# Two of four key blocks of the first attention turned by VectorE and through DRAM, and twelve weight units split in the first down-projection

## The chip, the cores and the metric

The kernel runs on one core of a Trainium2 chip. A core has a matrix engine (TensorE, PE in the profile; PEld is its loading of weights), VectorE (DVE), ScalarE (ACT), GpSimd (POOL), and SyncE (SP), which here only starts DMA transfers. Each engine works through its own list of instructions and waits for the others at semaphores. The metric is the device time of one execution in microseconds (us); lower is better.

## The reference

Two sequences of 512 tokens of width 1024 go through one encoder layer. Cut to what matters here:

```python
x = x + 0.5 * swiglu(rms_norm(x, ffn1_norm), w_gate, w_up, w_down)     # d_ff 2816
h = rms_norm(x, mix_norm)
aq, ak, av, mq, mk, mv, gate_pre, o_pre, g_att, g_mlstm = split(h @ w_in)
s = einsum('bqkgd,bskd->bkgqs', q, k) * scale                          # 8 heads, 512 x 512 each
p = softmax(s, axis=-1)
att = einsum('bkgqs,bskd->bqkgd', p, v)
mem = mlstm_bidirectional(mq, mk, mv, gate_pre, o_pre)                 # 4 heads
merged = sigmoid(g_att) * (att @ w_up_att) + sigmoid(g_mlstm) * (mem @ w_up_mlstm)
x = x + merged @ w_out
x = x + 0.5 * swiglu(rms_norm(x, ffn2_norm), ...)                      # then a last rms_norm
```

## The kernel before

All large products are done with operands split in two: a rounded value `hi` and a remainder `lo = x - hi`; a product is three matmuls (hi hi, hi lo, lo hi). So each weight that comes from DRAM is split first: ScalarE copies it to `hi`, VectorE subtracts to get `lo`. A *weight unit* is 128 columns of `w_in` over all 1024 rows, 512 KB; its split is one ScalarE and one VectorE instruction on 128x1024 elements (`split_w`, L278 and L279). `load_w` does this on the first use of a unit, and writes `hi` and `lo` to DRAM (`wpark`, twice 512 KB); on a later use under the same key in `parked` it loads both from there and splits nothing.

The program runs: first gate and up projection, first down-projection (`ffn_down`), `mix(0, ...)` for the first sequence, `mix(1, ...)` for the second, and the second feed-forward block. `ffn_down` works in 28 steps. Steps 0 to 13 and 21 to 27 have 36 matmuls of 128x512, steps 14 to 20 have 24. In each, four PSUM banks are filled one after the other (`d` from 0 to 3), and each is read out by one ScalarE or VectorE instruction (`flush_`, L663, L665). Four banks hold the X group (`mm`, `mm`, `mm`, `pso`) and four the Y group (`pss`, `pss`, `pst`, `pst`), so the next step of the same group can only start on a bank when its last flush is done. `prep` splits the weights of the step two further on (L715, L716).

`mix` has the attention. `score` makes one 128x512 block of probabilities: matmuls (L1101), a maximum (L1104), the exponential (L1106), the reciprocal (L1107), and the scaling of the rows, on ScalarE (L1109) or on VectorE (L1111). `values` multiplies them with V, for which each probability block must be turned, keys to the partitions. In `mix(0)`, `turn_keys` does this for all four key blocks with four TensorE transposes each (L1117) and a split of the result (`parts`). In `mix(1)` only key blocks 2 and 3 go this way. Blocks 0 and 1 are turned in 32x32 squares by VectorE (`turn_early`, L1129) into `turned`, which is rows 0 and 1 of the `box` tile; SP writes them to DRAM (`send`, L1133, `abuf`), and POOL's queue reads them back a head later in the order that completes the turn (`fetch`, L1138). `among(n)` puts `n` matmuls of waiting weight units between these steps. Twelve units of 24 matmuls each are used up in this way: those of `mem_qk(1, .)`, `att_gate(0)` to `att_gate(5)` and `out_gate(0)` to `out_gate(3)`.

The order on each engine is fixed when the program is built, by a scheduler that sorts by priority (program order, moved by `shifted`) and by what it takes to be ready; `pin` keeps marked instructions in program order.

Of the kernel before, what the change touches and what calls it, by code (L numbers as in the profile page):

```python
# [8 lines left out]
F32 = mybir.dt.float32  # L9
F32R = mybir.dt.float32r  # L10
# [16 lines left out]
def encoder(ctx, tc, I, outs):  # L27
# [519 lines left out]

    def ffn_down(wd, rb, ring, tail, xres, done, at_step, hook, turned=None):
# [4 lines left out]
        e5 = A([P, DH, S], F32, "e5")  # L553
        right = [[t[:, q] for q in range(3)] for t in rt] + [[t[:, 3] for t in rt]]
# [5 lines left out]
        s1s = ring.rows["s"]  # L560
        at = [0, 0]

        def load_right(i):
# [144 lines left out]

    def normed(xt, g, R, d):
# [138 lines left out]
    def mix(s, xh, xl, early=None, extra=None, after=None):  # L848
# [248 lines left out]
        def score(h, b):  # L1097
            hk = h // 4
            p = PS()
            for j in range(2):  # L1100
                pin(nc.tensor.matmul(p, qT[:, h, b * P:(b + 1) * P], kv[:, hk * 2 + j, :],  # L1101
                                     start=(j == 0), stop=(j == 1)))
# [4 lines left out]
            V_.reciprocal(c[:, 2:3], c[:, 1:2])  # L1107
            if b % 2 and (s or h or b < 3):
                nc.scalar.activation(e, e, AF.Copy, scale=c[:, 2:3])  # L1109
            else:  # L1110
                V_.tensor_scalar(e, e, c[:, 2:3], None, op0=ALU.mult)  # L1111
            return e

        def turn_keys(Ps, kb):
            p = PT()
            for b in range(4):
                pin(nc.tensor.transpose(p[:, b * P:(b + 1) * P], Ps[b][:, kb * P:(kb + 1) * P], ident))  # L1117
            return parts(p.rearrange("p (i a m) -> p a i m", i=4, a=4) if s else p)

# [21 lines left out]
        pos = {}  # L1141
        KBS = (2, 3, 0, 1) if s else (0, 1, 2, 3)

        def values(h, kb, pp):
# [5 lines left out]
            if kb != KBS[3]:  # L1150
                return
            po = pos.pop(h)
            order = ((lambda t: t.rearrange("p (a i m) -> p i a m", i=4, a=4)),
                     (lambda t: t.rearrange("p (i a m) -> p i a m", i=4, a=4))) if s else (lambda t: t,) * 2
            if h % 2 == 0:
# [30 lines left out]
        for b in range(4):  # L1186
            Ps.append(score(0, b))
            next(rope, None)
            among(FIRST[b])
        if s:  # L1190
            for i in range(2):
                turn_early(Ps[i], i)
        last = None
        for h in range(HA):
            nxt = []
            for b in range(4):
# [8 lines left out]
                if h + 1 < HA:  # L1205
                    nxt.append(score(h + 1, b))
                if s and (h, b) != (HA - 1, 3) and b in (3, 0):
                    if b == 3:
                        for i in range(2):
                            turn_early(nxt[i], i)  # L1210
                    else:
                        for i in range(2, 4):
                            turn_early(Ps[i], i)
                if s and b == 1:
                    send(h)
                n0, n1_ = FILLER if b else SOON
                among(n0)
                pp = None
                if not s or b > 1:
                    pp = h, b, turn_keys(Ps, b)  # L1220
# [8 lines left out]
            Ps = nxt  # L1229
        for b in range(2 * s):  # L1230
            pp = HA - 1, b, fetch(HA - 1, b)
# [520 lines left out]

    ffn_down(I["ffn1_w_down"][0], rbuf[0], up.ring, tail, xbuf, done1, 7, mix_consts)

# [201 lines left out]
```

## Time and profile before

| | us |
|---|---|
| median of 3 runs (2034.21 to 2035.5) | 2035.04 |
| profiled execution, its own time | 2037.6 |
| its span, first to last instruction | 2035.8 |
| first gate and up projection, about | 0 to 437 |
| first down-projection | 437 to 640 |
| `mix(0)` up to its attention | 640 to 705 |
| attention of `mix(0)`, first to last score matmul (L1101) | 705 to 803 |
| attention of `mix(1)`, up to its last score matmul | to 1169 |

The granted clock of TensorE is 0.999 over the span. The profile has no instruction of `fetch`, `send` or `turn_early` ahead of 1080 us: in the kernel before only `mix(1)` uses them. In rows of the profile a time in front is the start within the span; "x4" counts instructions; a bracket says how long the engine was idle before the row and whose instruction ended the wait.

### The profile page before, as it was taken

The numbers are of one execution on the slowest core, as the hardware profiler recorded it, in microseconds if no ns is written. First come the engines' busy times: TensorE is split into PE (matmuls) and PEld (weight loads), VectorE is DVE, ScalarE is ACT, GpSimd is POOL, SyncE is SP. The second block draws the span as 40 slices with busy tenths as digits, with TensorE's granted clock in tenths as the row PEclk, the third lists the DMA queues.
The fourth block names the chain that finished last, engine by engine and source line by source line (L and its number), as shares of the span: only waits on it lengthen the run. The fifth ranks groups of instructions, "written<-read, shape, count | busy, mean of one in ns | idle before, by whom it ended". The sixth has DMA issues, their size and how long they took to land.

```text
span 2035.8 us, 26777 instructions
## 1 busy us (share of the span) xinstructions
PE 2020.2 (99%) x9185; PEld 1665.7 (82%) x9185; DVE 1584.0 (78%) x2828; ACT 921.5 (45%) x1675; POOL 111.1 (5%) x148
## 2 busy tenths in 40 slices
PE   9999999999999999999999999999999999999998
PEld 7888888888888888888888877888888888888887
DVE  7988888886797798776566867467798988786797
ACT  7644444442234577653325654245444444442224
POOL 0000000001003000100120000011000000000001
PEclk9999999999999999999999999999999999999999
DMA  9656565799766954868656668877565655689753
GB/s 312 197 171 216 177 218 182 237 334 364 271 214 225 294 169 148 259 208 302 211 166 209 214 189 268 274 228 228 173 206 166 217 177 179 205 332 352 269 196 119
DMA packets 334696, 462.17 MB, mean 227 GB/s; under 512 B 21384, under 2 KB 207840, under 8 KB 333280
## 3 DMA queue, kind: packets, MB, share of 16 engines
q1 hardware_dynamic: 329920, 446.08, 65.8%
q0 software_dynamic: 4480, 14.11, 2.0%
q8 instruction: 72, 1.18, 0.2%
q14 instruction: 64, 0.52, 0.1%
q10 hardware_dynamic: 160, 0.27, 0.0%
HBM read 292.44 MB, written 167.94 MB: 226 GB/s over the span
## 4 chain that ended last, share of the span: by engine, by line
PE 91%; DVE 3%; DMA 3%; ACT 2%; issue 1%; SPq 0%; DVEq 0%; ACTq 0%
PE mm L839 13%; PE pso L374 12%; PE pst L374 12%; PE mm L374 10%; PE mm L632 9%; PE pss L374 6%; PE pst L632 4%; PE pss L632 4%; PE mm L825 4%; PE mm L804 3%; PE pso L632 3%; PE pso L1148 1%; PE pss L1101 1%; PE pst L839 1%; PE pss L839 1%; PE pso L1360 1%
## 5 line engine op out<-in xcount | busy, mean ns | idle before, releaser
L374 PE MATMUL pst<-xc,w 128*128 128x512 f32 x1056 | 253.8, 389 | 1.2 <-ACT t L409 1.2
L374 PEld LDWEIGHTS pst<-xc,w 128*128 128x128 f32 x1056 | 198.1, 188 | 42.7 <-ACT t L409 1.6
L374 PE MATMUL mm<-xc,w 128*128 128x512 f32 x972 | 229.6, 390 | 1.6 <-ACT f L382 1.6
L374 PEld LDWEIGHTS mm<-xc,w 128*128 128x128 f32 x972 | 182.0, 188 | 39.6 <-ACT f L382 2.1
L632 PE MATMUL mm<-rt,w 128*128 128x512 f32 x765 | 178.7, 389 | 0.0
L839 PE MATMUL mm<-xh,w 128*128 128x512 f32 x560 | 176.1, 391 | 1.4 <-DMA w<-wpark 1.4
L332 ACT ACTIVATE w<-t 128x512 fp32r<-128x512 f32 x176 | 106.5, 627 | 135.7 <-issue 63.1
L632 PEld LDWEIGHTS mm<-rt,w 128*128 128x128 f32 x765 | 143.5, 188 | 29.8
L333 DVE TENSOR_TENSOR w<-t,w 128x512 fp32r<-128x512 f32 x176 | 117.8, 688 | 40.9 <-ACT w L332 39.1
L374 PE MATMUL pso<-xc,f 128*128 128x512 f32 x528 | 127.0, 389 | 0.0
L374 PE MATMUL pss<-xc,w 128*128 128x512 f32 x528 | 126.8, 389 | 0.0
L374 PE MATMUL pso<-xc,w 128*128 128x512 f32 x528 | 126.8, 389 | 0.0
L839 PEld LDWEIGHTS mm<-xh,w 128*128 128x128 f32 x560 | 104.8, 188 | 23.7 <-DMA w<-wpark 1.8
L374 PEld LDWEIGHTS pso<-xc,f 128*128 128x128 f32 x528 | 99.0, 188 | 21.0 <-DVE t L413 0.4
L374 PEld LDWEIGHTS pso<-xc,w 128*128 128x128 f32 x528 | 99.1, 188 | 20.6
L374 PEld LDWEIGHTS pss<-xc,w 128*128 128x128 f32 x528 | 99.1, 188 | 20.6
L825 PE MATMUL mm<-xh,w 128*128 128x512 f32 x336 | 111.9, 398 | 0.0
L839 PE MATMUL mm<-xl,w 128*128 128x512 f32 x280 | 109.6, 391 | 0.0
L715 ACT ACTIVATE w<-wr 128x512 fp32r<-128x512 f32 x72 | 45.1, 632 | 138.4 <-PE pso L632 64.8
L278 ACT ACTIVATE w<-wr 128x1024 fp32r<-128x1024 f32 (+1 forms) x64 | 65.3, 1030 | 80.4 <-issue 24.5
L279 DVE TENSOR_TENSOR w<-wr,w 128x1024 fp32r<-128x1024 f32 (+1 forms) x64 | 79.8, 1247 | 26.6 <-ACT w L278 15.7
L715 ACT ACTIVATE w<-t 128x512 fp32r<-128x512 f32 x82 | 51.8, 632 | 107.4 <-PE pst L632 62.4
(457 smaller groups left out, 4080.4 us busy)
## 6 DMA issues: line engine op xcount, KB each, us to landing
rt<-rbuf SPq DMA_DIRECT2D x154, 512.0 KB, 5.4
wpark<-w SPq DMA_DIRECT2D x88, 512.0 KB, 3.6
w<-wpark SPq DMA_DIRECT2D x88, 512.0 KB, 5.3
wr<-in_ffn_w_gate_dram SPq DMA_DIRECT2D x62, 512.0 KB, 5.4
rbuf<-tab SPq DMA_DIRECT2D x102, 256.0 KB, 4.0
wr<-in_ffn_w_up_dram SPq DMA_DIRECT2D x44, 512.0 KB, 4.6
rbuf<-f SPq DMA_DIRECT2D x72, 256.0 KB, 4.2
wr<-in_w_in_dram SPq DMA_DIRECT2D x36, 512.0 KB, 5.7
```

The costliest lines, as they stand in the source:

```text
L278: pin(nc.scalar.activation(hi, raw, AF.Copy))
L279: pin(lo_eng.tensor_tensor(lo, raw, f(hi), op=ALU.subtract))
L332: pin(nc.scalar.activation(t[:, 0], src, AF.Copy))
L333: pin(V_.tensor_tensor(t[:, 1], src, f(t[:, 0]), op=ALU.subtract))
L374: nc.tensor.matmul(p, a[:, k, :], xt[:, b, k, :], start=(first and k == 0 and i == 0), stop=(k == HK_ - 1 and i == 2), skip_group_check=True)
L632: nc.tensor.matmul(p, u[:, a, d * P:(d + 1) * P], r[:, b, ts], start=(first and q == 0 and k == 0), stop=(q == len(us) - 1 and k == 2), sk ...
L715: nc.scalar.activation(hi, src, AF.Copy)
L804: mark(nc.tensor.matmul(p[b][:, :N], a[:, k, bs], w_[:, kl, :], start=(k == 0 and i == 0), stop=(k == KD - 1 and i == 2)), (kl, b, i) == ( ...
L825: pin(nc.tensor.matmul(p[0], a[:, k, :], b, start=(k == 0 and i == 0), stop=(k == n - 1 and i == 2)))
L839: mark(nc.tensor.matmul(p, a[:, k, :], b, start=(k == 0 and i == 0), stop=last), last)
L1101: pin(nc.tensor.matmul(p, qT[:, h, b * P:(b + 1) * P], kv[:, hk * 2 + j, :], start=(j == 0), stop=(j == 1)))
L1148: pin(nc.tensor.matmul(pos[h], Vst[:, kb, h // 4, :], w, start=(kb == KBS[0] and i == 0), stop=(kb == KBS[3] and i == 1)))
```

## The change

In `mix(0)` key blocks 0 and 1 now go the way that they go in `mix(1)`, and the blocks are taken in the order 2, 3, 0, 1. From its second head on, all rows of `mix(0)` are scaled on ScalarE. And `ffn_down` gets a list `aside` of twelve weight units of `w_in`: the ones named above. The half of the tile `e5` that was unused holds one unit at a time (`spare`: `lo` and `hi`). `split_aside` loads a unit on POOL's queue, splits it on ScalarE (L569) and VectorE (L570), and writes both halves to `wpark` on POOL's queue (L574). The unit is entered in `parked`, so that `mix(0)` loads it split. One unit is written into the program after each step from 10 on. Only the first `ffn_down` gets a list.

```diff
+        e5_ = A([P, KD, S], F32, "e5")
+        e5, spare = e5_[:, 0:DH], e5_[:, DH:KD].rearrange("p (i a) c -> p i (a c)", i=2)
...
+        def split_aside(view, key):
+            lo, hi = [spare[:, i].rearrange("p (k c) -> p k c", c=view.shape[2]) for i in range(2)]
+            nc.gpsimd.dma_start(lo, view)
+            nc.scalar.activation(hi.bitcast(F32R), lo, AF.Copy)
+            V_.tensor_tensor(lo.bitcast(F32R), lo, hi, op=ALU.subtract)
+            shape = [P, 2] + list(view.shape[1:])
+            parked[key] = d, _ = dpool.tile(shape, F32, name=nm("wpark")), shape
+            for i, t in enumerate((hi, lo)):
+                nc.gpsimd.dma_start(d[:, i], t)
...
+            if i >= ASIDE and aside:
+                split_aside(*aside.pop(0))
+
+    ASIDE = 10
...
-            if b % 2 and (s or h or b < 3):
+            if b % 2 and (s or h or b < 3) or not s and h:
                 nc.scalar.activation(e, e, AF.Copy, scale=c[:, 2:3])
...
-        KBS = (2, 3, 0, 1) if s else (0, 1, 2, 3)
+        KBS = 2, 3, 0, 1
...
-        if s:
-            for i in range(2):
-                turn_early(Ps[i], i)
+        for i in range(2):
+            turn_early(Ps[i], i)
...
-                if s and b == 1:
+                if b == 1:
                     send(h)
...
-                if not s or b > 1:
+                if b > 1:
                     pp = h, b, turn_keys(Ps, b)
                 elif h:
                     pp = h - 1, b, fetch(h - 1, b)
...
+             aside=[(win_v[:, :, c:c + P], ("in", c)) for c in
+                    (896, 1408, *(2832 + d * P for d in range(2)), *(2320 + h * P for h in range(HM)),
+                     *(2832 + d * P for d in range(2, 6)))])
```

On VectorE, in the first down-projection: before, the flushes of step 3 (`pss_3890` to `pst_3923`) have weight remainders (`w`) among them.

```order
L716 TENSOR_TENSOR w_3695<-t_7_268,w_3695 128x512
L665 SCALAR_TENSOR_TENSOR xs_3693<-pss_3890,xs_3693 128x512
L665 SCALAR_TENSOR_TENSOR xs_3693<-pss_3901,xs_3693 128x512
L665 SCALAR_TENSOR_TENSOR xs_3693<-pst_3912,xs_3693 128x512
L716 TENSOR_TENSOR w_3695<-t_8_269,w_3695 128x512
L716 TENSOR_TENSOR w_3696<-wr_3702,w_3696 128x512
L665 SCALAR_TENSOR_TENSOR xs_3693<-pst_3923,xs_3693 128x512
```

In the changed program the same place reads (`e_276` is the tile of `spare`):

```order
L733 TENSOR_TENSOR w_3695<-t_7_268,w_3695 128x512
L678 SCALAR_TENSOR_TENSOR xs_3693<-pss_3890,xs_3693 128x512
L678 SCALAR_TENSOR_TENSOR xs_3693<-pss_3901,xs_3693 128x512
L678 SCALAR_TENSOR_TENSOR xs_3693<-pst_3912,xs_3693 128x512
L570 TENSOR_TENSOR e_276_3694<-e_276_3694 128x1024
L678 SCALAR_TENSOR_TENSOR xs_3693<-pst_3923,xs_3693 128x512
L733 TENSOR_TENSOR w_3695<-t_8_269,w_3695 128x512
L733 TENSOR_TENSOR w_3696<-wr_3702,w_3696 128x512
```

The third of the twelve subtractions stands between the third and the fourth flush of step 3, and so not after step 10, where the program text has the first. All twelve stand between the second flush of step 1 and the last flush of step 15.

On POOL, at the same time: before, only the constants of `mix` are prepared there (`tab`, `gb`).

```order
L744 DMA tab_4218<-in_c_tri_dram 128x512
L745 DMA tab_4218<-in_c_mask_dram 128x256
L747 DMA f_302_4221<-in_c_rope_dram 128x8x64
L750 DMA gb_4223<-in_q_norm_dram 128x64
L752 TENSOR_SCALAR gb_4223<-gb_4223 128x64
L754 TENSOR_TENSOR tab_4218<-f_302_4221,gb_4223 128x256
```

Now the loads (L568) and stores (L574) of the twelve units stand on POOL, the first two units and the third load ahead of these rows, and then, from the fifth unit on:

```order
L568 DMA e_276_3694<-in_w_in_dram 128x8x128
L574 DMA wpark_4613<-e_276_3694 128x1024 x2
L568 DMA e_276_3694<-in_w_in_dram 128x8x128
L574 DMA wpark_4657<-e_276_3694 128x1024 x2
L568 DMA e_276_3694<-in_w_in_dram 128x8x128
L574 DMA wpark_4701<-e_276_3694 128x1024 x2
```

Each load writes the tile that the two stores ahead of it read, so the units follow one another without overlap.

On TensorE, in the attention of `mix(0)`: before, between the value products (`pso`) of two key blocks stand the four transposes (`ident`) of another, among matmuls of a weight unit (`mm`) and a score (`pss`).

```order
L1117 MATMUL pst_6154<-ident,t_484_5964 128x128
L1117 MATMUL pst_6154<-ident,t_491_5994 128x128
L1117 MATMUL pst_6154<-ident,t_503_6043 128x128
L1117 MATMUL pst_6154<-ident,t_509_6072 128x128
L825 MATMUL mm_6119<-xh_4898,w_6006 128x512
L825 MATMUL mm_6119<-xl_4899,w_6006 128x512
L825 MATMUL mm_6119<-xh_4898,w_6006 128x512
L1148 MATMUL pso_6166<-t_521_6128,kv_5279 128x512
L1148 MATMUL pso_6166<-t_522_6129,kv_5279 128x512
```

Now, between the products of key block 3 (`t_504`, `t_505`) and of block 0 (`t_513`, `t_514`):

```order
L1165 MATMUL pso_6122<-t_504_6115,kv_5351 128x512
L1165 MATMUL pso_6122<-t_505_6116,kv_5351 128x512
L1118 MATMUL pss_6160<-kv_5351,qT_5354 128x512 x2
L842 MATMUL mm_6146<-xl_4971,w_6050 128x512
L842 MATMUL mm_6146<-xh_4970,w_6050 128x512 x2
L842 MATMUL mm_6146<-xl_4971,w_6050 128x512
L842 MATMUL mm_6146<-xh_4970,w_6050 128x512 x2
L842 MATMUL mm_6146<-xl_4971,w_6050 128x512
L842 MATMUL mm_6146<-xh_4970,w_6050 128x512
L1165 MATMUL pso_6122<-t_513_6152,kv_5351 128x512
L1165 MATMUL pso_6122<-t_514_6153,kv_5351 128x512
```

No transposes stand there any more; 64 of them are gone from the attention of `mix(0)`.

More of the change, by code (lines that the diff above doesn't have):

```diff
@@ L546, in encoder, with ffn_down @@
     n_steps = len(DOWN) * len(CHUNKS)
-    def ffn_down(wd, rb, ring, tail, xres, done, at_step, hook, turned=None):
+    def ffn_down(wd, rb, ring, tail, xres, done, at_step, hook, turned=None, aside=()):
         n = n_steps
@@ L561, in ffn_down @@
         at = [0, 0]
+        aside = list(aside)
+        def split_aside(view, key):
[7 more added lines that the diff above has]
+                nc.gpsimd.dma_start(d[:, i], t)
         def load_right(i):
@@ L1206, in mix @@
                     nxt.append(score(h + 1, b))
-                if s and (h, b) != (HA - 1, 3) and b in (3, 0):
+                if (h, b) != (HA - 1, 3) and b in (3, 0):
                     if b == 3:
@@ L1229, in mix @@
             Ps = nxt
-        for b in range(2 * s):
+        for b in range(2):
             pp = HA - 1, b, fetch(HA - 1, b)
```

7 lines of the change are left out of this document (3 added, 4 removed).

## The prediction

> **What bounds the kernel now.** I read the page first: the span, the engines' busy times and the chain that ended last.
>
> ```profile
> span 2035.8 us, 26777 instructions
> PE 2020.2 (99%) x9185; PEld 1665.7 (82%) x9185; DVE 1584.0 (78%) x2828; ACT 921.5 (45%) x1675; POOL 111.1 (5%) x148
> PE 91%; DVE 3%; DMA 3%; ACT 2%; issue 1%; SPq 0%; DVEq 0%; ACTq 0%
> ```
>
> TensorE is busy for 2020.2 of 2035.8 us and makes 91% of the chain. So a TensorE instruction taken out is worth its whole time, work taken off VectorE or ScalarE is worth nothing as such, and whatever makes TensorE wait is paid in full: only 15.6 us of the span are idle, so there is no later gap in which a delay could vanish. Next the windows by stage; the columns are the window, the busy time of PE, PEld, DVE, ACT and POOL, the granted clock, the DMA engines' busy share and GB/s. The first three rows are the down-projection, the start of `mix(0)`, and its attention with what follows it, the next two the attention of `mix(1)` and what follows there, the last three are pieces of the down-projection.
>
> ```profile
> 437.00:640.00 203.00, 203.00 (x898) 168.06 (x897) 159.74 (x247) 64.91 (x107) 18.15 (x19) 1.00 0.75 269
> 640.00:705.00 65.00, 65.00 (x340) 55.40 (x339) 47.08 (x99) 32.47 (x55) 13.73 (x21) 1.00 0.91 302
> 705.00:870.00 165.00, 164.75 (x802) 133.35 (x801) 138.37 (x296) 112.28 (x226) 5.89 (x4) 1.00 0.61 202
> 1080.00:1180.00 100.00, 99.24 (x473) 80.77 (x472) 78.08 (x185) 65.18 (x136) 8.77 (x16) 1.00 0.66 202
> 1180.00:1347.00 167.00, 164.94 (x721) 133.48 (x720) 105.20 (x283) 69.57 (x161) 8.56 (x16) 1.00 0.77 245
> 454.00:462.40 8.40, 8.40 (x39) 6.96 (x38) 2.79 (x6) 3.83 (x8) 0.00 (x0) 1.00 1.04 409
> 486.90:495.00 8.10, 8.10 (x37) 6.70 (x37) 7.96 (x13) 2.28 (x5) 1.71 (x2) 1.00 1.04 405
> 544.00:552.20 8.20, 8.20 (x38) 6.79 (x37) 5.75 (x10) 1.93 (x4) 0.00 (x0) 1.00 0.66 226
> ```
>
> In the stages that the change touches TensorE has no gap. The DMA engines are full up to about 495 us (409 and 405 GB/s) and have room after it (226).
>
> **The transposes that go.** Sixty-four of the 128 in `mix(0)` (the first row) go: 8 heads, 2 key blocks, 4 each.
>
> ```profile
> L1117 PE MATMUL pst<-ident,t x128: 270/272/329, 717.6 to 811.4; 128*128 128x128 f32 x128
> 1094.45 0.60 PE L1117 MATMUL pst<-ident,t 128*128 128x128 f32 x4
> ```
>
> One is recorded with 272 ns, but matmuls overlap: four in a row end after 0.60 us, so each takes (0.60 - 0.27) / 3 = 0.11 us of TensorE. 64 x 0.11 = 7.0 us. Since TensorE is the bound there, they come off the time. That they were hidden before, so that the change would do nothing, is excluded by the 164.75 of 165.
>
> **The rest of the attention.** These rows price what moves on VectorE and ScalarE: the splits of a unit, a turn, and the scaling of rows on either engine.
>
> ```profile
> L279 DVE TENSOR_TENSOR w<-wr,w 128x1024 fp32r<-128x1024 f32 x60 | 76.1, 1270 | 25.9 <-ACT w L278 15.0 <-DMA wr<-in_w_out_dram 9.7 <-DMA wr<-in_w_in_dram 0.5
> L278 ACT ACTIVATE w<-wr 128x1024 fp32r<-128x1024 f32 x60 | 62.7, 1055 | 76.5 <-issue 24.5 <-PE mm L839 12.9 <-PE mm L804 11.3
> L1129 DVE STREAM_TRANSPOSE box<-t x32: 393/428/446, 1080.8 to 1172.8; 128x256 f32<-128x256 f32 x32
> L1111 DVE TENSOR_SCALAR t<-t,asm 128x512 f32<-128x512 f32 x33 | 16.0, 485 | 0.8
> L1109 ACT ACTIVATE t<-t,asm 128x512 f32<-128x512 f32 x31 | 22.3, 719 | 1.4 <-DVE asm L1107 1.2
> ```
>
> VectorE loses 12 x 1.27 = 15.2 us of splits and 14 x 0.485 = 6.8 of scaling, and gets 32 x 0.43 = 13.7 of turns: 8.3 us less. ScalarE loses 12 x 1.06 = 12.7 and gets 14 x 0.72 = 10.1. Neither becomes the bound. But the way through DRAM adds three waits. The sends stand in SP's list with the loads of units behind them; the value products of the last head wait for a fetch with little left to put between; and the first memory head loads its gates into the `box` rows that `turned` holds until the last send. `mix(1)` has all three. The first row below has the 64 scores of `mix(0)`, the others are of `mix(1)` and of the whole trace.
>
> ```profile
> L1101 PE MATMUL pss<-kv,qT x64: 387/393/500, 705.6 to 802.9; 128*128 128x512 f32 x64
> 1113.31 5.62 SPq L293 DMA_DIRECT2D w<-wpark  x3
> 1127.55 1.84 SPq L1133 DMA_DIRECT2D abuf<-box  x4
> 1194.37 6.63 DMA box<-ebuf
> w<-wpark SPq DMA_DIRECT2D x88, 512.0 KB, 5.3
> ```
>
> There, TensorE loses 0.76 us in the attention and 2.06 after it (windows above), though the 6.63 us of the gates' load are on the chain. In `mix(0)` a unit lasts about three scores, 97.3 us / 32 x 3 = 9.1 us, and less the 2 x 3 transposes that go (0.7 us) about 8.4 from now on; its two loads take 5.3 us and the second issue, some 6. Some two us are left, and four sends hold SP for 1.84. I take 4 us for all three waits; the ends are 0 (all hidden) and 20 (each of eight sends costs its 1.84 us, and the chain of the gates' load 5).
>
> **The units in the down-projection.** Here the order decides. The load of a unit waits for the stores of the one before, so a unit takes one full round: load, 1.06 us on ScalarE, 1.27 on VectorE, store. The order shows where the twelve subtractions stand: behind the second flush of step 1, and, for the last, behind the third flush of step 15. The first row has the first three flushes of step 1 (the second ends at about 452.3), the second row those of X banks up to step 15, of which the last starts at 561.7 and ends at 562.4; the others show TensorE at step 15 and the two steps after it.
>
> ```profile
> 450.88 2.06 DVE L665 SCALAR_TENSOR_TENSOR xs<-mm,xs 128x512 f32<-128x512 f32 x3
> L665 DVE SCALAR_TENSOR_TENSOR xs<-mm,xs x15: 678/691/692, 450.9 to 561.7; 128x512 f32<-128x512 f32 x15
> 557.61 4.08 PE mm L632 x18
> 561.69 1.36 PE pso L632 x6
> 563.05 2.72 PE pss L632 x12
> 568.49 2.72 PE pss L632 x12
> ```
>
> So eleven rounds must fit into about 562.4 - 452.3 = 110 us, 10.0 us each. If a round takes longer, ScalarE and VectorE stand still at the unit, and behind it in their lists stand the flush that frees a PSUM bank for the next step, and the weights of a step soon due: behind the last one those of step 17, which TensorE begins at 568.49. That gives some 5.5 us of slack, once. What TensorE loses is 11 x round - 110 - 5.5, so a round of **10.5 us** is the point from which it loses. No row shows such a round, so I bound it by the loads of units and the stores to `wpark`, of the same size, that SP issues in `mix(0)`: each row has the issues, and the line behind it the shortest, median and longest time from issue to landing. The first two pairs are of 640 to 705 us, at 302 GB/s, the others of 705 to 870 us, at 202 GB/s.
>
> ```profile
> L271 SPq DMA_DIRECT2D wr<-in_w_in_dram x12: 432/791/2553, 643.7 to 694.3; - x12
> DMA to landing us min/median/max: 5.3/6.9/8.4
> L303 SPq DMA_DIRECT2D wpark<-w x26: 319/339/1370, 639.8 to 704.3; - x26
> DMA to landing us min/median/max: 2.6/4.6/6.4
> L271 SPq DMA_DIRECT2D wr<-in_w_in_dram x17: 384/452/1826, 705.0 to 866.9; - x17
> DMA to landing us min/median/max: 4.4/5.1/6.7
> L303 SPq DMA_DIRECT2D wpark<-w x40: 319/320/706, 706.9 to 866.5; - x40
> DMA to landing us min/median/max: 2.6/3.5/5.0
> ```
>
> The quiet stage gives 5.1 + 3.5 + 2.33 = 10.9 us, the busy one 6.9 + 4.6 + 2.33 = 13.8. The shortest landings give 4.4 + 2.6 + 2.33 = 9.3, the longest 8.4 + 6.4 + 2.33 = 17.1. The twelve units bring 12 x 1.5 MB = 18.9 MB, some 120 GB/s while they run, on top of what the stretch moves now, so it is nearer to the busy stage. And POOL's own queue is slow there: these two waits are for transfers of 32 KB.
>
> ```profile
> 477.30 0.37 POOL L752 TENSOR_SCALAR gb<-gb 128x64 f32<-128x64 f32 x1 [6.84 <-DMA gb<-in_q_norm_dram]
> 486.02 0.73 POOL L754 TENSOR_TENSOR tab<-f,gb 128x256 f32<-128x256 f32 x1 [5.14 <-DMA gb<-in_k_norm_dram]
> ```
>
> I take 13.4 us, a little below the busy stage because a TensorE that waits also asks for less: 11 x 13.4 = 147.4, less 115.5, makes **32 us** lost. The ends are 0 (9.3) and 11 x 17.1 - 115.5 = 73 us. A gain here is excluded: TensorE has 203.00 of 203.00 us.
>
> The Trainium skill, "DMA: Bandwidth & Descriptors", section "Anatomy of one DMA — SWDGE (gpsimd) path", prices a transfer that GpSimd issues at about 2.0 us and its bytes at 436 GB/s. By it a 512 KB transfer is estimated at 3.2 us, a round at 8.7, and nothing would be lost. The trace doesn't agree in this stretch: the same formula gives some 2.1 us for the two 32 KB transfers, and POOL waited 5.14 and 6.84.
>
> **The sum**, against the profiled execution: 2037.6 - 7.0 + 4 + 32 = 2066.6 us. Its own time is 2.6 us above the median of the runs (2035.0), so 2064.
>
> **Rivals.** *The round keeps pace.* If loads and stores land in nearly their shortest times, a round is 9.3 to 10.5 us, ScalarE and VectorE never wait long, and only the attention counts: 2035.0 - 7.0 + 0 to 4 = 2028 to 2032, faster. It decides at 10.5 us. For it: the shortest landings, and that POOL's queue holds only the units, where SP's transfers stand behind others. (By the rule of the Trainium skill quoted above it would come out this way.) Against it: every median and the two waits of POOL. Chance 0.17. *The round is just too long,* 10.8 to 12.4 us as in the quiet stage: 3 to 21 us lost, 2035 to 2053. For it: from 495 us on the DMA engines have room. Chance 0.20, of which 0.05 lies within 0.2% (4 us) of before. *The forecast,* 12.4 to 14.8 us: 21 to 47 lost, 2053 to 2079. Chance 0.45. *The DMA engines stay full,* because 4.7 MB of the first three units fall into the stretch at 400 GB/s, the loads of the steps' own operands come late too, or the waits of the attention reach their upper end: 2079 to 2105. For it: the window rows at 1.04. Chance 0.18.
>
> **How the numbers follow.** The predicted time is the forecast's, 2064. The range from 2030 to 2090 holds the forecast, the rounds just too long, a third of the case that keeps pace, and about half of the last; about 2 in 10 are left out. What differs by less than 0.2% is about what a measurement of this kernel can't tell from no change. Faster by more: 0.17; within it: 0.05; slower: 0.78.
>
> **What the profile after would show.** Right: between about 455 and 600 us TensorE is idle ahead of L645 (the matmuls of `ffn_down`, L632 before), released by VectorE's flush or a weight's split; ScalarE is idle ahead of L569, released by the DMA of `w_in`; the twelve starts of L570 lie 12 to 15 us apart; the down-projection lasts 220 to 250 us where it took 203; the attention's 64 scores take some 7 us less. Wrong: starts of L570 about 10 us apart and TensorE without a gap; or a gap in the attention ahead of L842 (a unit's weights late) or L1165 (a fetch late) of more than 4 us in sum.

## The result, and the profile after

The changed kernel takes 2096.6 us (median of 4 runs, 2094.36 to 2098.76) beside 2034.85 us for the kernel before: a ratio of 1.0301, with a 95% interval of 1.0289 to 1.0313. It is slower, as predicted, but 32.6 us slower than the predicted 2064, and beyond the range, which ended at 2090.

The first lines of the page after, and the row of its slices with TensorE's granted clock:

```profile
span 2096.7 us, 26806 instructions
PE 2035.1 (97%) x9121; PEld 1672.5 (80%) x9121; DVE 1581.1 (75%) x2846; ACT 928.6 (44%) x1689; POOL 141.6 (7%) x200
PEclk9999999998889999999999999999999999999999
```

TensorE executes 64 instructions less and is nevertheless busy 14.9 us longer (2035.1 beside 2020.2), and 61.6 us of the span are idle where 15.6 were. The clock falls in three slices, which lie in the first down-projection. The windows show where all of it is. The same stages of the kernel before (columns as in the prediction): from the first matmul of the down-projection to the first of the projection of `mix(0)`, the 64 scores, and from the last score to the first transpose of the memory's output.

```profile
437.90:647.50 209.60, 209.60 (x928) 173.56 (x927) 164.97 (x263) 66.93 (x111) 18.51 (x21) 1.00 0.75 271
705.60:802.90 97.30, 97.05 (x483) 79.00 (x482) 87.85 (x182) 70.03 (x138) 0.00 (x0) 1.00 0.51 172
802.90:832.30 29.40, 29.40 (x140) 23.79 (x139) 21.06 (x47) 21.55 (x46) 2.04 (x1) 1.00 0.58 208
```

and in the changed kernel, with two pieces of its down-projection behind them:

```profile
437.90:707.10 269.20, 227.73 (x922) 183.81 (x921) 171.28 (x274) 75.67 (x122) 40.69 (x57) 0.90 0.80 280
765.20:856.00 90.80, 90.42 (x427) 73.45 (x426) 74.79 (x175) 68.48 (x140) 6.74 (x13) 1.00 0.63 197
856.00:894.20 38.20, 32.27 (x133) 24.52 (x132) 24.57 (x54) 24.02 (x49) 3.16 (x5) 0.91 0.62 206
486.00:494.00 8.00, 2.16 (x5) 1.78 (x6) 4.04 (x6) 3.25 (x5) 1.93 (x4) 0.63 1.01 358
510.00:518.00 8.00, 8.00 (x25) 6.37 (x26) 6.50 (x11) 2.25 (x5) 1.57 (x3) 0.67 0.46 169
```

The windows of the down-projection start at the same time in both, but in the changed kernel its first matmul comes at 436.8 us, 1.0 us sooner than before. So it ends 59.6 us later and is 60.6 us longer: 41.5 us in which TensorE stands, and 19.1 in which it runs the same matmuls more slowly. The scores take 6.5 us less, and the piece behind them gives back 8.8. The two short pieces show the two kinds of loss: between 486 and 494 us TensorE works 2.16 of 8 us; between 510 and 518 it is busy throughout, but at a clock of 0.67 gets 25 matmuls done. The prediction's row of 18 matmuls in 4.08 us makes 0.227 us each, by which 8 us have room for 35.

The waits behind it, in the trace's sums of waits in the down-projection (engine, line, what released it; us in all, times, the longest), first ScalarE's and VectorE's, then POOL's:

```profile
ACT e L569 <- DMA e<-in_w_in_dram: 121.0, 11, 15.8
DVE e L570 <- ACT e L569: 90.8, 11, 15.3
POOL e L568 <- DMA wpark<-e: 42.3, 10, 7.8
```

And the units' own rows: the twelve subtractions, and the landing of the loads and then of the stores (shortest, median, longest):

```profile
L570 DVE TENSOR_TENSOR e<-e x12: 1218/1225/1226, 451.1 to 624.7; 128x1024 fp32r<-128x1024 f32 x12
DMA to landing us min/median/max: 4.4/7.9/10.9
...
DMA to landing us min/median/max: 2.9/4.7/8.5
```

Eleven rounds take 624.7 - 451.1 = 173.6 us, 15.8 each, where 13.4 was predicted, and in each of them ScalarE and VectorE stand for a while. How that reaches TensorE is seen in the timelines (start, us, what; in brackets the idle time ahead and its releaser), first two rows of VectorE, then TensorE's:

```profile
489.96 1.23 DVE L570 TENSOR_TENSOR e<-e 128x1024 fp32r<-128x1024 f32 x1 [14.32 <-ACT e L569]
491.10 0.69 DVE L678 SCALAR_TENSOR_TENSOR xs<-pst,xs 128x512 f32<-128x512 f32 x1
...
491.84 3.73 PE L645 MATMUL pst<-rt,w 128*128 128x512 f32 x9 [8.74 <-DVE xs L678]
509.78 6.96 PE L645 MATMUL mm<-rt,w 128*128 128x512 f32 x18 [4.01 <-ACT e L676]
523.31 2.37 PE L645 MATMUL mm<-rt,w 128*128 128x512 f32 x9 [0.45 <-DVE xs L678]
601.31 4.21 PE L645 MATMUL pso<-rt,w 128*128 128x512 f32 x9 [3.77 <-DVE e L678]
612.82 1.68 PE L645 MATMUL pso<-rt,w 128*128 128x512 f32 x6 [2.19 <-DVE xs L678]
614.31 5.89 PE L645 MATMUL mm<-rt,w 128*128 128x512 f32 x18
```

The releasers are flushes (L676, L678), which stand in the lists behind a unit that is waiting: VectorE waits 14.32 us for the unit's `hi`, subtracts, does the flush behind it, and only then do TensorE's 8.74 us end. Nine matmuls take 2.37 us after a wait of 0.45, but 3.73 and 4.21 after waits of 8.74 and 3.77.

### The profile page after: what moved, and what is told of

It reads as the page before. It is cut to its first block, busy times and chain, and to the rows that moved or that the text cites. A ratio compares the mean times of both kernels' runs of the same rounds, so it can differ in the third digit from the quotient of the medians.

```text
span 2096.7 us, 26806 instructions
## 1 busy us (share of the span) xinstructions
PE 2035.1 (97%) x9121; PEld 1672.5 (80%) x9121; DVE 1581.1 (75%) x2846; ACT 928.6 (44%) x1689; POOL 141.6 (7%) x200
## 4 chain that ended last, share of the span: by engine, by line
PE 84%; DMA 6%; DVE 4%; issue 3%; ACT 3%; POOL 0%; SPq 0%; ACTq 0%; DVEq 0%; POOLq 0%
PE mm L856 14%; PE pso L374 11%; PE pst L374 11%; PE mm L374 10%; PE mm L645 6%; PE pss L374 6%; PE mm L842 4%; PE pss L645 3%; PE pst L645 3%; PE mm L821 3%; DMA e<-in_w_in_dram 2%; DMA wpark<-e 2%; PE pso L645 2%; PE pss L1118 1%; PE pso L1165 1%
## 5 line engine op out<-in xcount | busy, mean ns | idle before, releaser
L645 PE MATMUL mm<-rt,w 128*128 128x512 f32 x765 | 187.1, 401 | 10.7 <-issue 6.3
L645 PEld LDWEIGHTS mm<-rt,w 128*128 128x128 f32 x765 | 149.0, 195 | 43.8 <-issue 6.7
L332 ACT ACTIVATE w<-t 128x512 fp32r<-128x512 f32 x176 | 106.5, 627 | 135.5 <-issue 63.1
L645 PE MATMUL pst<-rt,w 128*128 128x512 f32 x396 | 97.0, 398 | 14.3 <-DVE xs L678 8.7
L645 PE MATMUL pss<-rt,w 128*128 128x512 f32 x396 | 95.9, 395 | 6.0 <-ACT w L732 6.0
L645 PEld LDWEIGHTS pst<-rt,w 128*128 128x128 f32 x396 | 76.4, 194 | 31.2 <-DVE xs L678 9.2
L645 PEld LDWEIGHTS pss<-rt,w 128*128 128x128 f32 x396 | 75.7, 192 | 22.8 <-ACT w L732 6.8
```

Source lines behind the costliest of these rows:

```text
L332: pin(nc.scalar.activation(t[:, 0], src, AF.Copy))
L645: nc.tensor.matmul(p, u[:, a, d * P:(d + 1) * P], r[:, b, ts], start=(first and q == 0 and k == 0), stop=(q == len(us) - 1 and k == 2), sk ...
```

## The experiments

All are of the changed kernel unless it says otherwise; a down-projection's length is from its first matmul to the first of the projection of `mix(0)`, read as in the windows above.

**The attention alone.** The list of units to be split aside is left out of the call:

```
-    ffn_down(I["ffn1_w_down"][0], ..., mix_consts, aside=[...])
+    ffn_down(I["ffn1_w_down"][0], ..., mix_consts)
```

> Only the attention part of the change; the twelve units are split in mix(0) as before. Round theory (the loss of the change comes from rounds of load, split and store in line with ScalarE's and VectorE's lists): the down-projection takes 209.6 us as before; the attention saves 6.6 us up to its last score as in the changed kernel, its end gives 9 back, and VectorE, at 88 of 97 us before, gets 13.7 - 6.8 us more without losing the splits, so a few us more: 2036 to 2046. Rival (the attention part itself costs most of the 62 us, by way of VectorE or the transfers through DRAM): over 2060.

2041.7 us, ratio 1.0034 (1.0021 to 1.0047). The down-projection is as before, so all the rest of the change's loss hangs on the units. But the 7 us of the transposes aren't there either. Its scores, and the piece behind them:

```profile
703.90:800.70 96.80, 93.75 (x432) 73.72 (x431) 87.84 (x194) 78.39 (x151) 7.53 (x14) 1.00 0.80 253
800.70:836.50 35.80, 31.08 (x129) 23.93 (x128) 24.14 (x52) 22.84 (x48) 2.43 (x4) 0.90 0.57 192
```

TensorE's busy time falls to 93.75 us, yet the scores take 96.8: with the units' splits still there VectorE is busy 87.84 us, as before, and in the trace's sums TensorE waits 2.6 us for VectorE's instructions, beside 0.2 in the changed kernel.

**The units alone.** The attention's edits are undone for `mix(0)`:

```
-        KBS = 2, 3, 0, 1
+        KBS = (2, 3, 0, 1) if s else (0, 1, 2, 3)
...
-        for b in range(2):
-            pp = HA - 1, b, fetch(HA - 1, b)
+        for b in range(2 * s):
+            pp = HA - 1, b, fetch(HA - 1, b)
```

> Only the twelve units in the down-projection; the attention as before, all four key blocks by TensorE. Round theory: the down-projection takes about 269 us as in the changed kernel, and nothing is won later, since TensorE had no gap there: 2092 to 2098. Rival (attention part costs most): under 2060.

2090.41 us, 1.0272 (1.0257 to 1.0288), a little below the expectation. The down-projection takes 267 us (from 436.0 to 703.1); the scores 96.3, with TensorE busy for all of it. So neither part by itself shortens the scores by more than 1 us: in one case TensorE's own work fills them, in the other TensorE waits for VectorE, and only both together give 90.8.

**The transfers alone.**

```
             nc.gpsimd.dma_start(lo, view)
-            nc.scalar.activation(hi.bitcast(F32R), lo, AF.Copy)
-            V_.tensor_tensor(lo.bitcast(F32R), lo, hi, op=ALU.subtract)
...
-            for i, t in enumerate((hi, lo)):
+            for i, t in enumerate((lo, lo)):
```

> As the changed kernel, with the same bytes moved by POOL's queue in the down-projection (each unit loaded once, stored twice), but neither ScalarE nor VectorE touches the units, so no wait for them stands in these lists; both stored halves are the unsplit weights, so the output isn't the reference's. Round theory: the down-projection is back at 210 to 214 us, all 2036 to 2042. DMA rival (18.9 MB more on full DMA engines delay the steps' own operands, and the order is innocent): the loss stays, 2080 or more; in between, the share of each can be read.

2065.82 us, 1.0145 (1.0127 to 1.0163): between the two expectations. The down-projection's window is the first line; the second is from TensorE's timeline, the third from ScalarE's, the fourth TensorE's only long wait besides, in its sums:

```profile
436.10:672.60 236.50, 213.72 (x928) 175.54 (x927) 159.87 (x263) 66.26 (x110) 40.71 (x57) 0.96 0.87 319
644.24 3.73 PE L643 MATMUL pst<-rt,w 128*128 128x512 f32 x9 [18.43 <-DVE e L676]
639.18 2.56 ACT L143 ACTIVATE xh<-xs,gain 128x512 fp32r<-128x512 f32 x4 [26.26 <-DMA wpark<-e]
PE mm L643 <- issue: 2.5, 1, 2.5
```

Besides this one there is one of 1.8 us for `rt`, an operand of the steps; what ended the 2.5 us the profile doesn't show. The main one comes at the very end: ScalarE stands 26.26 us at the first normalisation for `mix(0)` (`xh`) until the last store of a unit has landed, and behind it in its list stand the weights of the last steps. The twelve loads start from 436.8 to 630.0, so a round takes 17.6 us even without ScalarE and VectorE, and the DMA engines stay full far longer than before the change. This is the piece from 520 to 540 us, in which the kernel before has them at 0.80 and 279 GB/s:

```profile
520.00:540.00 20.00, 20.00 (x90) 16.57 (x89) 10.79 (x17) 4.31 (x7) 3.11 (x5) 1.00 1.04 397
```

**Each load tied to a step.**

```
+            G_.tensor_copy(lo[:, 0, 0:1], behind)
             nc.gpsimd.dma_start(lo, view)
...
+    ASIDE = 1, 3, 5, 7, 9, 11, 13, 16, 19, 21, 23, 25
```

Here `behind` is a column of the accumulator that the last flush of the step wrote.

> As the changed kernel, but the load of each unit waits (by one POOL copy of one column) for the last flush of a step: 1, 3, 5, 7, 9, 11, 13, 16, 19, 21, 23, 25. So the rounds start 13 to 16 us apart and the scheduler puts each split behind its own step. Round theory: lateness no longer adds up; each round may still cost its own excess over what the scheduler reckons for a load, 0 to 2 us: down-projection 210 to 230 us, all 2034 to 2060. DMA rival: the same 18.9 MB in the same stage cost nearly the same, over 2075.

2092.6 us, 1.0285 (1.0267 to 1.0302): the expectation failed. The step held the load back, but the split stayed right behind its load in ScalarE's list:

```profile
ACT e L571 <- DMA e<-in_w_in_dram: 109.9, 11, 17.8
```

That is nearly the 121.0 of the change. More room between the units is of little use (4 us of 62) where a unit's own load gets none of it. The rival's number is met, so this run doesn't tell the two theories apart.

**Each split tied to a step, its load free.**

```
             nc.gpsimd.dma_start(lo, view)
+            nc.scalar.activation(hi[:, 0, 0:1], behind, AF.Copy)
             nc.scalar.activation(hi.bitcast(F32R), lo, AF.Copy)
...
+    ASIDE = 2, 4, 6, 8, 11, 13, 15, 17, 19, 21, 23, 25
```

> The whole change, but each unit's split on ScalarE is tied behind the last flush of steps 2, 4, 6, 8, 11, 13, ... 25 of the down-projection (a copy of one column that it overwrites), while its load goes as soon as the stores of the unit before have landed. So a round has two steps, about 15 us, and ScalarE and VectorE should find the unit already there. Theory A (what costs is the wait in the lists of ScalarE and VectorE, because a round of 15.8 us stood at places 10 us apart): at most 1 us of wait for each of 11 units is left, the down-projection takes 210 to 222 us instead of 269 and the time is 2037 to 2050 us. Rival B (what costs is that 18.9 MB more pass the DMA engines, and the steps' own operands come late whatever the order): the down-projection takes 235 us or more, as with the transfers alone, and the time is 2062 us or more.

2070.41 us, 1.0175 (1.0157 to 1.0194): 26 us better than the change with the same units, traffic and work, but far from 2050 and in rival B's region. The longest wait comes from late stores. TensorE's row, and the sum for ScalarE, whose column copy writes into `hi` and so waits for the stores of the unit before:

```profile
519.32 6.65 PE L647 MATMUL mm<-rt,w 128*128 128x512 f32 x18 [14.00 <-DVE e L682]
ACT e L570 <- DMA wpark<-e: 11.8, 1, 11.8
```

VectorE had ended that unit's split at 487.4 us, but POOL issued its two stores only at 499.98: in its list they stand behind the constants of `mix`, which wait for their own loads. The next unit's load goes at 510.26, when the stores have landed, and ScalarE waits another 8.78 us for it. So without the tie the split would have waited for the same load.

**The transfers alone, late.** The transfers alone, with the tie of the fourth run at steps 8, 9, 11, 12, 14 and so on.

> The transfers alone as before (the same loads and stores on POOL's queue, no work of ScalarE or VectorE on the units, both stores from the loaded tile, so that the stored halves are unsplit weights), but each load is tied by a POOL copy of one column behind the last flush of steps 8, 9, 11, 12, 14, ... 25, so that none falls into the stretch up to 495 us in which the DMA engines are full without them. Theory A1 (the 25 us that the transfers alone cost come from that full stretch: operands of the steps fall behind there): nothing of it is left, 2033 to 2042 us. Rival B (it is the sum of the bytes: the room after 495 us is 130 GB/s, which 18.9 MB in 130 us fill again): a single long stall stays, late in the down-projection, 2055 to 2068 us.

2079.44 us, 1.021 (1.0189 to 1.023), worse than either expectation; it decides nothing about the traffic. The copies on POOL read an accumulator, and stand in POOL's list behind stores; VectorE's next addition into that accumulator waits for the copy:

```profile
606.47 0.69 DVE L667 TENSOR_TENSOR xs<-xs,e 128x512 f32<-128x512 f32 x1 [6.11 <-POOL e L569]
625.72 0.69 DVE L667 TENSOR_TENSOR xs<-xs,e 128x512 f32<-128x512 f32 x1 [18.55 <-POOL e L569]
```

From 600 to 620 us TensorE works 7.13 us and the DMA engines are at 0.56, so it isn't they that hold it.

**Work kept back for the attention's end.** On the attention alone:

```
                 n0, n1_ = FILLER if b else SOON
+                n1_ -= not s and b > 0 and 0 < h < 7
...
-        among(FILLER[0])
+        among(FILLER[0] + (0 if s else 10))
```

with 4 more in each of the two calls ahead.

> The attention's part of the change alone (units split in mix(0) as before), with one matmul less of the gates' projections between the scores of heads 1 to 6 in mix(0) and the 18 kept for the end, where the last head's blocks go through DRAM. Theory A2 (at the attention's end TensorE lacks work to put under the send, fetch and split of the last head): the end from the last score to the first transpose of the memory's output shrinks from 35.8 us by 3 to 5 once the 18 x 0.23 = 4.1 us of moved work are left out, and the time falls from 2041.7 to 2036 to 2039 us. Rival: the scores are paced by ScalarE and VectorE, so fewer matmuls between them only make TensorE wait there: 2040 to 2044 us.

2043.91 us, 1.004 (1.0025 to 1.0055): no gain. The scores take 93.7 us instead of 96.8, the piece behind them 40.4 instead of 35.8 with 4.1 us of moved work in it. The wait for the last head's fetch is still 2.99 us of 4.3, since its blocks land only 6.38 us after the fetch, beside 3.88 in the attention alone. That the scores got 3.1 us shorter when some 4 us of TensorE's work left them also shows that in the attention alone VectorE isn't the only one to set the pace.

**The transfers alone, the norm's sums on VectorE.**

```
-        accs[s] = sq_add(xs[s][:, d, :], accs[s], "R")
+        accs[s] = sq_add(xs[s][:, d, :], accs[s], "R", eng=V_)
```

> The transfers alone, as in the third run (same loads and stores on POOL's queue, no ScalarE or VectorE work on the units, both stores from the loaded tile, so that the stored halves are unsplit weights), with one thing more changed: the additions of the squares' sums for the norm behind the first down-projection (L155) stand on VectorE instead of POOL. In the third run TensorE's one long wait of 18.4 us came while these additions stood in POOL's list behind the last units' stores and loads, ScalarE's normalisation behind them, and the weight splits of the last steps behind that. Theory A (POOL's list, not the DMA engines, made the transfers alone cost 25 us): that wait goes, and some 4 us of short waits stay: 2036 to 2047 us. Rival B (18.9 MB more in the DMA engines cost it): 2058 us or more.

2065.77 us, 1.0149 (1.0134 to 1.0165): the same as with the sums on POOL. It is rival B's number, but TensorE's one long wait, 18.97 us, makes most of it again. So the sums in POOL's list weren't the cause. ScalarE's row names it, as it did in the third run:

```profile
640.79 2.56 ACT L143 ACTIVATE xh<-xs,gain 128x512 fp32r<-128x512 f32 x4 [25.80 <-DMA wpark<-e]
```

`xh` is the next tile of the pool in which `spare` is a part of `e5_`. It takes over that memory, and must wait for the last store out of it.

**Nine units, each behind a step.** The tie goes through a tile of its own; the norm's sums stand on VectorE as above:

```
+            one = tied[:, len(parked):len(parked) + 1]
+            nc.scalar.activation(one, behind, AF.Copy, scale=0.0, bias=1.0)
-            nc.scalar.activation(hi.bitcast(F32R), lo, AF.Copy)
+            nc.scalar.activation(hi.bitcast(F32R), lo, AF.Copy, scale=one)
...
+    ASIDE = 9, 11, 13, 15, 17, 19, 21, 23, 25
```

> Nine of the twelve units in the down-projection (the last three are split in mix(0) as before), each split tied behind the last flush of steps 9, 11, ... 25, through a scale column of ones that ScalarE writes from that flush, in a tile of its own, so that no wait for a store hangs on the tie (the tie of the earlier run wrote into the unit's own tile and waited up to 11.8 us for its stores). The norm's additions stand on VectorE. A round now has two steps, some 14.9 us, lies behind the full stretch, and its load goes ahead on POOL's list. Theory A (only waits in the lists cost): 0 to 1 us for each unit, the down-projection takes 208 to 222 us, the time is 2033 to 2046 us, with nine units' traffic of 14.2 MB unchanged. Rival B (bytes): three quarters of what the transfers alone cost, 2055 us or more.

2055.35 us, 1.0096 (1.008 to 1.0113): theory A's number failed, and rival B's was met. The down-projection lost 13.3 us, less than the some 20 that are three quarters of what it lost to the transfers alone (26.9); the rest of the loss lies behind it. The down-projection's window, and two of the nine splits on ScalarE:

```profile
436.80:659.70 222.90, 213.59 (x927) 175.65 (x926) 172.79 (x273) 77.80 (x129) 26.89 (x39) 0.98 0.88 316
570.21 1.15 ACT L572 ACTIVATE e<-e,tied 128x1024 fp32r<-128x1024 f32 x1 [6.82 <-DMA e<-in_w_in_dram]
612.78 1.15 ACT L572 ACTIVATE e<-e,tied 128x1024 fp32r<-128x1024 f32 x1
```

That is 13.3 us for nine units, where the change loses 60.6 for twelve. Five of the nine splits still wait for their load (19.5 us in all): two steps of 7.5 us hold a round only just. By itself this run doesn't settle between the two.

**The last head on TensorE.** On the attention alone:

```
-            pp = HA - 1, b, fetch(HA - 1, b)
+            pp = HA - 1, b, fetch(HA - 1, b) if s else turn_keys(Ps, b)
```

and no turn and no send for that head.

> The attention's part of the change alone, but the last head of mix(0) has all four key blocks turned on TensorE, so its value products wait for no send and fetch. Theory A2 (the last head's way through DRAM, 18 us from the last score with too little work beside it, is what the attention's end gives back): 8 more transposes cost 8 x 0.11 = 0.9 us, the wait of 4.3 us and some 1.5 us behind it go: 2036 to 2039 us, and the end from the last score to the first transpose of the memory's output takes 29 to 32 us instead of 35.8. Rival (the wait only changes its name, because ScalarE and VectorE are late with the splits there): 2040 to 2043 us.

2040.29 us (10 runs, 2036.49 to 2042.37), 1.0022 (1.0012 to 1.0031). The piece behind the scores is what was expected:

```profile
801.10:832.80 31.70, 29.58 (x136) 23.11 (x135) 22.96 (x48) 22.71 (x48) 2.09 (x2) 1.00 0.51 181
```

31.7 us beside 35.8, with TensorE's wait for the fetch gone. The whole time, though, lies only 1.4 us below that of the attention alone, and the two sets of runs overlap; that the 4 us reach the end is not shown.

**Six units, each behind a step.** The same tie as for the nine, `ASIDE = 6, 9, 12, 15, 18, 21`, the sums on POOL as they were.

> Six units in the down-projection, each split tied behind the last flush of steps 6, 9, ... 21 (through the column of ones in a tile of its own, as for the nine), the other six split in mix(0) as before; the attention is that of the change. A round now has three steps, some 22 us, more than the 15.8 us it took, and the last store lands before mix(0) first writes into the memory of the boxes. Theory A3 (a unit costs TensorE time only where its place in the lists comes before its round is over): no idle of TensorE at the units, the down-projection takes 209 to 213 us, the time is 2036 to 2041 us, of which most is the attention's end. Rival B (each unit costs by its bytes or by its work on ScalarE and VectorE, wherever it stands): half of the 60 us of the change, or at least half of the 25 us of the transfers alone: 2047 us or more.

2042.63 us, 1.0036 (1.0023 to 1.0049), 1.6 us above the expectation and 4.4 below the rival's 2047. Its down-projection, scores and the piece behind them:

```profile
436.80:647.00 210.20, 209.91 (x927) 173.61 (x926) 173.04 (x270) 74.93 (x123) 31.24 (x39) 1.00 0.88 314
705.10:801.20 96.10, 93.25 (x432) 73.89 (x431) 82.63 (x183) 75.09 (x148) 7.53 (x14) 1.00 0.72 229
801.20:837.70 36.50, 30.94 (x129) 23.92 (x129) 24.26 (x52) 22.81 (x48) 3.26 (x4) 0.91 0.56 190
```

210.2 us with TensorE busy for 209.91, beside 209.6 before: six units with their 9.4 MB and all their work cost next to nothing where each place comes later than its round. All their stores, and all loads but the first, fall behind 495 us, so what they would cost in the full stretch isn't tested. Nearly the whole loss of this run is the attention's end (36.5 us beside 29.4).

**The transfers of nine units alone.**

```
-            if i >= ASIDE and aside:
+            if i >= ASIDE and len(aside) > 3:
```

on the transfers alone.

> The transfers alone (as in the third run: both stores from the loaded tile, unsplit weights stored), but of the first nine units only, one right behind the other; the other three are split in mix(0). In the third and the eighth run TensorE's one long wait came because ScalarE's first normalisation for mix(0) (xh, L143) waited 26 us for the last store from the boxes, whose memory it takes over. Nine rounds of 17 us end at about 590 us, before mix(0) wants that memory at 608. Theory A3 (it is the end of the chain of rounds that costs, not the traffic): the long wait goes, waits of 3 to 6 us stay from late operands, 2036 to 2044 us. Rival B (bytes): three quarters of the 28 us, 2054 to 2060 us.

2045.32 us, 1.005 (1.0033 to 1.0067), 1.3 us above the expectation and 8.7 below the rival's. The down-projection takes 217.1 us, and `xh` starts without a wait for a store:

```profile
436.50:653.60 217.10, 212.45 (x927) 174.26 (x926) 163.49 (x264) 66.70 (x111) 34.56 (x48) 0.99 0.89 327
L143 ACT ACTIVATE xh<-xs,gain x8: 706/724/727, 615.1 to 639.9; 128x512 fp32r<-128x512 f32 x8
```

So 14.2 MB packed into the first three quarters of the stage cost 7.5 us by themselves (4.65 us in which TensorE stands, half of it for `rt`, and 2.85 of slower running), and the wait of 18 us belonged to the end of a chain of twelve rounds.

## Why the prediction failed in size

**The bound and the mechanism were right.** TensorE is the bound, there was no gap for a delay to vanish in, and a unit takes one round of load, split and store at a place in the lists that comes too early: without the units the down-projection is as before, and six units at later places cost it 0.6 us. The rows named beforehand are there: TensorE idle ahead of L645, ScalarE idle ahead of L569 by the DMA of `w_in`. The starts of L570 lie 15.8 us apart and the down-projection takes 270 us, beyond the named 12 to 15 and 220 to 250.

**The step that failed is the price of a round.** The prediction took 13.4 us, "a little below the busy stage because a TensorE that waits also asks for less". It is 15.8: by their medians the loads land in 7.9 us (6.9 in the busy stage), the stores in 4.7 (4.6), the two engines take 2.3, and 0.9 is what else lies between. The first three rounds begin in the stretch where the DMA engines are full, and take 19.4 us each (starts 451.1 and, three on, 509.3); the last eight take 14.4.

The discount for a waiting TensorE had the right sign, but it was taken off too low a price. The busy stage was the start of `mix(0)`, at 302 GB/s. In the down-projection, with TensorE running nearly undelayed up to 600 us, the transfers alone take 17.6 us a round, at 330 to 414 GB/s from 450 us on; in the change, where TensorE stands for 41.5 us, they take 13.5 (15.8 less the 2.3 of the two engines; its two stores go out 1.3 us apart, and there at once). And the rows of `mix(0)` were of SP's queue, while the units go by POOL's. The shortest landings are alike (4.4 and 2.9 us here, 4.4 and 2.6 there), but no run sends a unit's transfers from SP, so a share of the queue in the price stays open.

The prediction's own sum with the measured round gives 11 x 15.8 - 115.5 = 58.3 us, beside the 60.6 measured. That is 26.3 of the 32.6 us it was wrong by; what is left over for the slack, counted as 5.5, is 3.0 (173.6 - 110 - 60.6), which is 2.5 more. The time lies in the region of the rival in which the DMA engines stay full. Of its three reasons the first, the units in the full stretch, has by place 3 x (19.4 - 13.4) = 18.0 us of the 26.3. That is read from where the rounds lie; the run that was to keep the transfers out of this stretch decided nothing.

By the Trainium skill's formula in "DMA: Bandwidth & Descriptors", section "Anatomy of one DMA — SWDGE (gpsimd) path", quoted in the prediction, a 512 KB transfer is estimated at 3.2 us; the shortest of the loads here took 4.4, and the median 7.9.

**The slower clock needed no term.** TensorE's 19.1 us of slower running look like a cost of their own. But ScalarE waited for a load at eleven of twelve units, so the chain of rounds set the pace, and matmuls that ran slowly in between only filled time that was lost anyway. This is argued from the sum, which comes out without them (58.3 beside 60.6); no run has the rounds without the slower running. Where the rounds fit better they do count: with nine units 3.7 of the 13.3 us are slower running (213.59 beside 209.91 for the six units).

**The transposes: right in sum, with a condition that the prediction didn't see.** -7.0 was predicted and the scores came out 6.5 shorter. But the prediction let the transposes come off the time because TensorE is the bound, and counted work taken off VectorE as worth nothing. The attention alone, with the same transposes gone, gains 0.5 us: VectorE, busy for 87.84 of 96.8 us, then makes TensorE wait. The units' splits had to leave VectorE for the gain to appear.

**The waits of the attention** were put at 4 and are 8.8: the way of the last head through DRAM. The chain of the changed kernel there (start, us, what), and TensorE's wait at its end:

```profile
863.42 3.40 DMA abuf<-box
867.37 5.14 DMA f<-abuf
...
873.28 0.51 PE L1165 MATMUL pso<-t,kv 128*128 128x512 f32 x1 [4.24 <-ACT t L732]
```

5.9 us of it are idle and 2.9 slower running. One of the signs of being wrong is there: the prediction named more than 4 us of gaps ahead of L1165, and this one alone has 4.24. In the attention alone the piece is 6.4 us longer than before, and turning that head on TensorE took 4.1 of them off, which shows the cause for that part; the rest is open. The sends in SP's list and the gates' load, the other two waits of the prediction, show no long wait of TensorE.

**The sum.** 26.3 for the round, 2.5 for the slack, 4.8 for the attention's waits and 0.5 for the scores make 34.1 us, less the 1.0 by which the down-projection starts sooner 33.1, beside the 32.6 by which the prediction was short.

**What stands against twelve free units.** Twelve rounds in one tile must end before `mix(0)` takes its memory over, or ScalarE waits there as it did with the transfers alone. Its first normalisation (L143) starts at 608.9 us in the kernel before; from 437.5 us, when the first load goes, that leaves 14.3 us a round, less than the 15.8 measured and the 17.6 of the transfers alone. No version that ran beats the kernel before: six units at nearly no cost free too little of VectorE (scores 96.1), and the attention's end costs more than that. Twelve rounds short enough, and an attention's end without the wait beside them, were not tried.

## What to carry to other kernels

Work that is moved into a free stage must be priced by the round trip of its buffer, measured in that stage's own traffic, and by the place of each step in the engines' lists; free engine time and free bandwidth didn't show it here. Put the consumer of a load at least one full round behind its issue (here three steps, 22 us, for a round of 16), and ask when the buffer's memory is wanted next. A gain that is held by two engines at once appeared here only when both were relieved: test the parts of a change one at a time before adding their gains.

## What was not expected of the hardware

The granted clock fell after TensorE's waits, and some of 2.2 to 2.5 us were enough. Two rows are from the transfers of nine units alone, the third from the run with each load tied to a step:

```profile
506.26 5.04 PE L643 MATMUL mm<-rt,w 128*128 128x512 f32 x21 [1.70 <-DMA rt<-rbuf]
548.32 7.98 PE L643 MATMUL mm<-rt,w 128*128 128x512 f32 x27 [2.33 <-issue]
...
489.54 6.42 PE L647 MATMUL mm<-rt,w 128*128 128x512 f32 x27 [2.47 <-ACT e L680]
```

27 such matmuls take 6.28 us in the changed kernel where no wait stands ahead (at 527.56 us). After the wait of 1.70 us little or nothing is lost (21 x 0.227 = 4.8), after 2.33 us 1.7 us are, after 2.47 us only 0.1. In the changed kernel 2.19 us sufficed: the first six matmuls behind this wait take 1.68 us, but the next 18 take 5.89 where 18 take 4.24 at full clock (at 518.61 us). Behind each of its waits of 3.77 us and more the matmuls ran slower; a window of 8 us behind one had a clock of 0.67. The Trainium skill, "TensorE: Matmul & The Clock Gate", section "Part 1: The HAM clock gate (the "warmup" mystery)", says that after an idle window of about 3.4 us the array runs at half its clock, and is at full clock again after about as long of work. On the length the traces differ: waits of 2.19 and 2.33 us were enough. By its figures one such wait is estimated to cost 1.7 us of slower running, and that is what the wait of 2.33 us cost; the eight waits of 2.19 us and more in the down-projection of the change cost 19.1 / 8 = 2.4 us each.

A queue's landings spread widely within one stage. In the run of the transfers alone the loads and then the stores on POOL's queue, 512 KB each, landed after (shortest, median, longest):

```profile
DMA to landing us min/median/max: 4.5/7.8/8.7
...
DMA to landing us min/median/max: 2.9/7.6/12.9
```

So one store can take ten microseconds longer than another of the same size in the same stage, and a median from another stage is no bound.
